# Fixing the order of all five queues in branch B of the long sequence

## The chip, the cores and the metric

The kernel runs on one core of one Trainium2 chip. The metric is the device time of one launch in microseconds (us), from runs on the chip. Engines are named as the profile names them: PE is TensorE (PEld its weight loads), DVE VectorE, ACT ScalarE, POOL GpSimd, SP SyncE, which here only issues DMAs. A name with a q (SPq, ACTq) is the queue that issues a DMA.

## What is computed

One layer of an encoder with two token mixers, for two sequences, a short one of 512 tokens and a long one of 1024, each of width 1024:

```python
xn = _rmsnorm(x, norm_mix_g)
z  = xn @ w_in                      # -> q_A k_A v_A q_B k_B v_B gate_A gate_B
o_a = gqa_attention(...)            # branch A: all keys, rotary, 8 heads
o_b = neighbourhood_attention(...)  # branch B: tokens on a 64-wide grid, 8 rows x 16 columns
                                    # of keys around a query, a learned bias per head and offset
mix = (sigmoid(ga) * (o_a @ w_proj_a) + sigmoid(gb) * (o_b @ w_proj_b)) @ w_out
x = x + mix
x = x + relu(_rmsnorm(x) @ w_mlp_up)**2 @ w_mlp_down
```

and a last RMSNorm. All products are made in split form: each operand is a high part and a low part (the remainder), and a product is three matmuls (`mm3`). The high part is an ACT copy, the low part a DVE subtraction (`split`, here called a cut).

## The kernel before

`run` handles the short sequence (NB = 1), then the long one (NB = 2): phase R (projections of branch A), phase A (its attention), phase B (branch B's attention), phase G (gated merge and `w_out`). `mlp` follows for both. The change is in phase B of the long sequence.

Phase B goes in steps `i` of one unit each; a unit `u = (h, j)` is head `h` and strip `j` of 16 grid columns. There are `n = 32` units; the first 24 are `moved`: their probabilities are transposed by a detour through DRAM instead of on PE. What happens to a moved unit `u = units[i]`:

- step i: `s_unit` adds bias and mask (POOL, `bm`), computes the scores on PE into one of two big PSUM tiles, adds the bias and takes the minimum on DVE (L1049, below called the sums), then exp on ACT (L1075) into `pb`, of which there are two, and scales by 1/sum on POOL (L1078);
- step i+1: `turn`, a DVE transpose of 32x32 blocks (L1087), and `dump`, a DMA from ACT's queue to DRAM (`tbs<-pbs`, L1094);
- step i+2: `fetch_t`, four DMAs from SP's queue that bring the blocks back in turned order (`bhs<-tbs`, L1104);
- step i+3: `t_unit`, a high copy on ACT (L1115) and a low subtraction on DVE (L1116);
- step i+4: `v_unit`, six matmuls with the values into a PSUM tile (`obs`), then `finish_o`, which adds the two halves of that tile (ACT L470, DVE L471 and L483) and writes them to DRAM through `put`.

Between those, every step issues fill work on PE: pulls from the generator `gate` (three matmuls a pull, 16 pulls a chunk of 128 gate columns, tanh at the end of each half chunk), and in steps 5, 6 and 7 of every eight the projection `qkproj` of the next two heads. `prep_v` loads the value strips (SP, `vss<-vds`, L942). From step 25 on the fill is `proj_a`, the product with `w_proj_a` (`ppas`). Its first weights and its operands `oX` are loaded at step 21 and cut one after the other from the list `oa_held`, whose first entry (the cut of the first weight chunk, `w_pa`) is taken at the end of step 22.

PSUM has four tiles for everything but scores (`mm`): gate sums, projections, transposes and `obs` share them. Weight tiles of `proj_a` come from the left pool `s8l`, which has six slots; until branch B's gate is done, the six hold parts of the split input `xhl`, the first of them the first half of the first 512 tokens (`xs_0`, k = 0 to 3). Raw weights pass through three buffers (`rawp`).

The scheduler of the tile framework puts each engine's instructions in a queue order at compile time. Before the change PE's order was pinned to the source (`keep_in_program_order` while `held_pe` is set); on ACT, DVE and SP `note` and `behind` made a few instructions (exp, sums, fetches and strip loads) stay behind every cut or load traced since the last such point, and the rest was free. POOL was free.

Of the kernel before, what the change touches and what calls it, by code (L numbers as in the profile page):

```python
# [18 lines left out]
P = 128  # L19
D = 1024  # L20
NC8 = D // P
# [40 lines left out]
def encoder(ctx: ExitStack, tc: tile.TileContext, xs, outs, w):  # L62
# [120 lines left out]
    held_pe = []  # L183
    firm = {"ACT": [], "DVE": [], "SP": []}

    def note(engine, op):
        if held_pe:
            firm[engine].append(op.ins)

    @contextmanager  # L190
    def behind(engine):
        with ExitStack() as st:
            for ins in firm[engine]:
                st.enter_context(tc.issue_after(ins))
            yield
        firm[engine].clear()

    def split(hi, lo, src, pin=False):
        op = nc.scalar.activation(hi, src, AF.Copy)  # L199
        note("ACT", op)  # L200
# [4 lines left out]
        for a, b in zip(cut, cut[1:]):  # L205
            op = nc.vector.tensor_tensor(lo[:, a:b], src[:, a:b], hi[:, a:b].bitcast(F32), op=ALU.subtract)
            if pin:
                tc.keep_in_program_order(op)
            note("DVE", op)

    def mul(out, a, b, **kw):
        op = nc.tensor.matmul(out, a, b, **kw)  # L212
        if held_pe:
            tc.keep_in_program_order(op)
# [16 lines left out]
    def load_cols(src, off, ncol, name, alloc=None, pin=False, hold=None, raw_of=None):  # L231
# [9 lines left out]
        for k0 in range(0, nk, kp):  # L241
# [4 lines left out]
            note("SP", op)  # L246
# [172 lines left out]
    def run(tr, nxt, first):  # L419
# [19 lines left out]
        def gate(goff, dst, c0=0, c1=NC8):  # L439
# [3 lines left out]
            for c in range(c0, c1):  # L443
                wg = nxt_w
                held = []
                if c + 1 < c1:
                    nxt_w = load_cols(win, goff + (c + 1) * P, P, f"g{N}_{goff}_{c + 1}", hold=held)
# [393 lines left out]
        def load_o(br, hold=None, raw_of=raw_tile):  # L841
            parts = []
            for k in range(4 - br):
                raw = None

                def ask(k=k):
                    r = raw_of(f"rawo{N}_{br}_{k}")
                    note("SP", nc.sync.dma_start(r[:, :T], (oad, obd)[br][k * P : (k + 1) * P, :]))
                    return r
# [24 lines left out]
        def proj_a(pool, raw_of):  # L874
            nxt_w = load_cols(
                w["w_proj_a"][0], 0, P, f"pa{N}_0", slot_left, NB == 2, oa_held if NB == 2 else None, raw_of
            )
            oA = load_o(0, oa_held, raw_of)
            if NB == 1:
                oa_held.pop(0)()  # L880
            yield
            for c in range(NC8):
                wp = nxt_w
                if c + 1 < NC8:
                    nxt_w = load_cols(
                        w["w_proj_a"][0], (c + 1) * P, P, f"pa{N}_{c + 1}", slot_left, raw_of=raw_of
                    )
                else:
                    wp_b.append(load_cols(w["w_proj_b"][0], 0, P, f"pb{N}_0"))
                for tb in range(NB):  # L890
# [4 lines left out]
                    za = pool.tile([P, 512], F32, tag="za", name=f"za{N}_{c}_{tb}", bufs=2)  # L895
                    nc.sync.dma_start(za, zg[0][c * P : (c + 1) * P, cs])
                    for k in range(4):
                        while len(oa_held) > max(0, 2 - k):
                            oa_held.pop(0)()
                        mm3(p_, wp[k][0], wp[k][1], oA[k][:, 0, cs], oA[k][:, 1, cs], k == 0, k == 3)  # L900
# [3 lines left out]
                        mA[tb, c // 4][:, c % 4, :], za, 1.0, p_, op0=ALU.add, op1=ALU.mult  # L904
# [8 lines left out]
        with phase(f"phB{N}") as ph:  # L913
            msk = ph.tile([P, halves * 3, nkey], BF16, tag="msk", name=f"msk{N}", bufs=1)
            nc.gpsimd.dma_start(msk, w["mask2"] if halves == 2 else w["mask1"])
            rects, strips, bms, PT = {}, {}, {}, {}
# [38 lines left out]
            def qkproj(pr, wqk, dest):  # L955
# [4 lines left out]
                def queries(tb):  # L960
# [5 lines left out]
                    for e in range(2):  # L966
# [11 lines left out]
                        note("ACT", nc.scalar.activation(dst_h, src, AF.Copy, scale=0.125))  # L978
                        for jj in range(4):
                            op = nc.vector.scalar_tensor_tensor(  # L980
# [7 lines left out]
                            note("DVE", op)  # L988
# [29 lines left out]
            def s_unit(u, before=None):  # L1018
                h, j = u
                ct = (0, 1, 1, 2)[j]  # L1020
                c0 = (0, 8, 24, 32)[j]
                jr = (16, 8, 8, 0)[j]
                s = big(f"sb{N}_{h}_{j}")
                for hf in range(halves):
                    r0 = 0 if hf == 0 else 4
                    ir = 4 if hf == 0 else 0
                    if j != 2:
# [7 lines left out]
                        bms[hf] = bm  # L1035
                    q0 = j * (T // 4) + hf * P
                    so = s[:, hf * 512 : hf * 512 + nkey]
                    for i in range(2):
# [3 lines left out]
                        mul(so, qk[h // 2][0][:, h % 2, q0 : q0 + P], kv, start=(i == 0), stop=(i == 1))  # L1042
                sums = []
                for hf in range(halves):
# [3 lines left out]
                    with behind("DVE"):  # L1048
                        nc.vector.tensor_tensor_reduce(  # L1049
                            out=sb,  # L1050
                            in0=s[:, hf * 512 : hf * 512 + nkey],
                            in1=bms[hf],
                            op0=ALU.add,
                            op1=ALU.min,
                            scale=-1.0,
                            scalar=3e38,
                            accum_out=nm_,
                        )
                    sums.append((sb, nm_))
                if before is not None:  # L1060
                    before()
                ps = []
# [3 lines left out]
                for hf, (sb, nm_) in enumerate(sums):  # L1066
                    nm = f"{N}_{h}_{j}_{hf}"
                    l = sml.tile([P, 1], F32, tag="l", name=f"lb{nm}")
# [5 lines left out]
                    with behind("ACT"):  # L1074
                        nc.scalar.activation(to, of, AF.Exp, bias=nm_, scale=-1.0, accum_out=l)  # L1075
                    rl = sml.tile([P, 1], F32, tag="rl", name=f"rlb{nm}")
                    nc.vector.reciprocal(rl, l)
                    nc.gpsimd.tensor_scalar(p, p, rl, 1.0, op0=ALU.mult, op1=ALU.mult)  # L1078
                    ps.append(p)
                PT[u] = pm if u in moved else ps  # L1080

            def turn(u):
# [4 lines left out]
                tc.keep_in_program_order(nc.vector.transpose(blocks, blocks))  # L1087
# [891 lines left out]
```

## Time and profile before

| what | value |
|---|---|
| median of three runs | 2148.83 us (2147.6 to 2149.58) |
| profiled execution, its own time | 2150.11 us |
| its span, first to last instruction | 2148.2 us |
| mean granted PE clock | 0.995 |
| PE, DVE, ACT, POOL busy | 98%, 69%, 53%, 17% of the span |
| phase B of the long sequence, steps 0 to 33 | 798.6 to 1072.3 us |

Times in the trace count from the start of the span. An engine's idle time stands in brackets in a row of the timeline, with what ended it. The order of the steps on PE can be read from the scores (`sbs`), four matmuls at the head of each step: step 8 starts at 855.06, step 16 at 915.42, step 24 at 989.74, step 27 at 1026.11.

### The profile page before, as it was taken

The page shows a single profiled execution, that of the slowest core. Times are in us where ns is not written, and L with a number is a line of the kernel's source. Part 1 is how long each engine was busy: PE and PEld are TensorE (multiplying, and loading weights), DVE is VectorE, ACT ScalarE, POOL GpSimd, SP SyncE. Part 2 cuts the span into 40 slices and gives each one's busy share as a digit, 9 for nine tenths or more (in the row PEclk, how much of TensorE's full clock was granted, in tenths as well). Part 3 has the DMA queues.
Part 4 walks back from the last instruction along what each step waited for, and adds up shares of the span by engine and source line. Part 5 has one row for each costly group of instructions (what it writes and reads, how often), then busy time and mean ns, then how long its engine had stood idle before and what let it go on. Part 6 is the DMA issues. An engine that isn't in the chain of part 4 may idle for free.

```text
span 2148.2 us, 32018 instructions
## 1 busy us (share of the span) xinstructions
PE 2105.0 (98%) x10871; PEld 1842.7 (86%) x10871; DVE 1483.7 (69%) x2793; ACT 1143.3 (53%) x2487; POOL 359.8 (17%) x446
## 2 busy tenths in 40 slices
PE   9999999999999999997999999999999999999998
PEld 8888778988897888876888899999999988888886
DVE  6665786777657757666782877778777777759563
ACT  6664653767566645544540566566655643434352
POOL 2232310323233224423200200003000000000000
PEclk9999999999999999999999999999999999999999
DMA  6437557520222146576562665578444799788561
GB/s 190 133 98 206 159 162 248 187 69 26 62 75 66 42 108 191 180 211 180 178 225 111 213 196 179 181 236 218 152 154 153 252 355 336 219 276 282 169 201 63
DMA packets 338538, 372.94 MB, mean 174 GB/s; under 512 B 33472, under 2 KB 269640, under 8 KB 338376
## 3 DMA queue, kind: packets, MB, share of 16 engines
q1 hardware_dynamic: 296695, 296.17, 44.3%
q10 hardware_dynamic: 34528, 54.55, 7.1%
q0 software_dynamic: 7152, 20.19, 3.6%
q8 instruction: 86, 1.41, 0.3%
q14 instruction: 77, 0.62, 0.1%
HBM read 274.29 MB, written 97.32 MB: 173 GB/s over the span
## 4 chain that ended last, share of the span: by engine, by line
PE 64%; DMA 2%; DVE 2%; ACT 1%; issue 1%; SPq 1%; POOL 0%; ACTq 0%; POOLq 0%; DVEq 0%
PE dn L212 20%; PE ua L212 6%; PE ud L212 6%; PE uc L212 6%; PE gpss L212 4%; PE ops L212 4%; PE ub L212 3%; PE ppbs L212 2%; PE ppas L212 2%; PE dnf L212 2%; PE pqbs L212 2%; PE pTs L814 1%; PE pkbs L212 1%; DMA tbs<-pbs 1%; PE obs L212 1%
## 5 line engine op out<-in xcount | busy, mean ns | idle before, releaser
L212 PE MATMUL dn<-wd,ah 128*128 128x512 f32 x1248 | 384.4, 389 | 0.0
L212 PEld LDWEIGHTS dn<-wd,ah 128*128 128x128 f32 x1248 | 234.3, 188 | 48.6
L212 PE MATMUL dn<-wd,al 128*128 128x512 f32 x624 | 242.8, 389 | 0.0
L1453 ACT ACTIVATE ah<-ar 128x512 fp32r<-128x512 f32 x168 | 104.4, 628 | 200.9 <-PE dn L212 188.3
L212 PE MATMUL gpss<-xs_0h,w_gs 128*128 128x512 f32 x512 | 188.4, 403 | 5.0 <-ACT w_gs L199 4.2
L1454 DVE TENSOR_TENSOR al<-ar,ah 128x512 fp32r<-128x512 f32 x168 | 114.3, 688 | 76.4 <-ACT ah L1453 66.6
L212 PE MATMUL ud<-B,A 128*128 128x384 f32 x768 | 143.6, 334 | 0.8 <-DVE c L1571 0.8
L212 PE MATMUL uc<-B,A 128*128 128x384 f32 x768 | 143.7, 334 | 0.0
L212 PE MATMUL ua<-B,A 128*128 128x384 f32 x768 | 138.8, 334 | 0.0
L212 PEld LDWEIGHTS dn<-wd,al 128*128 128x128 f32 x624 | 117.2, 188 | 24.2
L780 POOL TENSOR_SCALAR ps<-ps,rls 128x1024 f32<-128x1024 f32 (+1 forms) x96 | 97.2, 1014 | 225.3 <-DVE rls L779 199.9
L212 PEld LDWEIGHTS ud<-B,A 128*128 128x128 f32 x768 | 133.9, 188 | 1.1 <-DVE c L1571 1.1
L212 PEld LDWEIGHTS uc<-B,A 128*128 128x128 f32 x768 | 134.1, 188 | 0.2 <-ACT A L1453 0.2
L212 PEld LDWEIGHTS ua<-B,A 128*128 128x128 f32 x768 | 133.7, 188 | 0.2
L820 DVE TENSOR_TENSOR ptls<-pTs,pths 128x512 fp32r<-128x512 f32 x160 | 107.6, 686 | 37.5 <-ACT pths L819 36.9
L819 ACT ACTIVATE pths<-pTs 128x512 fp32r<-128x512 f32 x160 | 94.2, 598 | 73.8 <-PE pTs L814 71.3
L212 PE MATMUL ops<-wh_os,mgs 128*128 128x512 f32 x384 | 119.4, 390 | 0.0
L774 DVE TENSOR_REDUCE nms<-ss 128x1 f32<-128x1024 f32 (+1 forms) x96 | 99.9, 1041 | 25.5 <-PE ss L772 25.0
L212 PEld LDWEIGHTS gpss<-xs_0h,w_gs 128*128 128x128 f32 x512 | 96.1, 189 | 24.4 <-ACT w_gs L199 5.1
L777 ACT ACTIVATE ps<-ss,nms 128x1024 f32<-128x1024 f32 (+1 forms) x96 | 93.3, 973 | 22.7 <-DVE nms L774 20.1
L180 POOL TENSOR_TENSOR rs_f<-ms_f,mhalf 128x1 f32<-128x1 f32 x6 | 4.0, 668 | 590.7 <-DVE ms_f L176 590.7
L814 PEld LDWEIGHTS pTs<-ident,ps 128*128 128x128 f32 x640 | 77.9, 140 | 28.6 <-POOL ps L780 4.5
(287 smaller groups left out, 5147.9 us busy)
## 6 DMA issues: line engine op xcount, KB each, us to landing
ar<-ud SPq DMA_DIRECT2D x120, 512.0 KB, 4.7
br<-in_w_mlp_down_dram SPq DMA_DIRECT2D x72, 512.0 KB, 5.1
rawu<-in_w_mlp_up_dram SPq DMA_DIRECT2D x64, 512.0 KB, 4.1
ud<-c ACTq DMA_DIRECT2D x128, 192.0 KB, 3.0
raw_gs<-in_w_in_dram SPq DMA_DIRECT2D x32, 512.0 KB, 4.0
ud<-cs SPq DMA_DIRECT2D x64, 192.0 KB
tbs<-pbs ACTq DMA_DIRECT2D x24, 384.0 KB, 3.8
bhs<-tbs SPq DMA_DIRECT2D x96, 96.0 KB, 2.9
```

Of the source, the lines that this page charges most:

```text
L180: nc.gpsimd.tensor_tensor(r[:, :n], m[:, :n], mhalf[:, :n], op=ALU.pow)
L212: op = nc.tensor.matmul(out, a, b, **kw)
L774: nc.vector.tensor_reduce(nm_, s, axis=AX.X, op=ALU.max, negate=True)
L777: nc.scalar.activation(p, s, AF.Exp, bias=nm_, accum_out=l)
L780: nc.gpsimd.tensor_scalar(p, p, rl, 1.0, op0=ALU.mult, op1=ALU.mult)
L814: nc.tensor.transpose(pt[:, j * P : (j + 1) * P], PP[u, j][:, kc * P : (kc + 1) * P], ident)
L819: nc.scalar.activation(hi, pt, AF.Copy)
L820: nc.vector.tensor_tensor(lo, pt, hi.bitcast(F32), op=ALU.subtract)
L1453: nc.scalar.activation(hi, src, AF.Copy)
L1454: nc.vector.tensor_tensor(lo, src, hi.bitcast(F32), op=ALU.subtract)
```

## The change

The notes and the pins of phase B go. A new function, `in_order`, is called at the end of every step and once after the loop; it adds to each instruction traced since its last call an order edge (no semaphore) behind the one traced before it on the same engine. So from the first step on PE, ACT, DVE, POOL and SP each issue in the order in which the source names them, DMA issues included. The source is rearranged with that:

- `s_unit` is split in `bias_sums`, `scores`, `sums`, `exps` and `scale`; in the long sequence the biases of unit i+1 are added in step i, and the dump stands directly behind the exp.
- `finish_o` of a `v_unit` is kept in a list `ends` and traced in the next step, behind that step's exp and scale.
- On SP a step now holds, in this order: fetches, puts of the step before, rectangles, value strips, weights.
- The cut of the next gate chunk moves from the third k of the chunk's first half to the second k of its second half.
- `proj_a` asks for weights up to three chunks ahead and cuts them one chunk ahead; `za` is asked for one half chunk ahead.
- In the steps from 22 on, the entry of `oa_held` at the end of a step comes before the `v_unit`s, not behind.
- The short sequence keeps its loop, written apart, with the same order in it.

The core of the diff:

```diff
+    def in_order(start=False):
+        traced = nc.cur_bb.bb.instructions
+        if start:
+            firm.append(traced[-1])
+            return
+        k = next(k for k in reversed(range(len(traced))) if traced[k] is firm[0])
+        for ins in traced[k + 1 :]:
+            if ins.engine in chained:
+                tc.add_manual_dep(ins, chained[ins.engine].name, ... NoSync ...)
+            chained[ins.engine] = ins
+        firm[0] = traced[-1]
...
-                        if k == 2:
-                            while held:
-                                held.pop(0)()
+                        if k == (1 if firm else 2) and tb == (NB - 1 if firm else 0):
+                            while cuts:
+                                cuts.pop(0)()
...
         def proj_a(pool, raw_of):
+            ask_w(0)
+            if NB == 1:
+                cut_w(0)
+            else:
+                oa_held.append(partial(cut_w, 0))
             oA = load_o(0, oa_held, raw_of)
+            if NB == 2: (entries 2 and 3 of oa_held also call ask_w(1), ask_w(2))
...
                     for k in range(4):
                         while len(oa_held) > max(0, 2 - k):
                             oa_held.pop(0)()
+                        if NB == 2 and k == 1:
+                            if (c, tb) != (NC8 - 1, 1):
+                                ask_z(c + tb, 1 - tb)
+                            if tb == 0:
+                                cut_w(c + 1)
+                                if c + 3 <= NC8:
+                                    ask_w(c + 3)
                         mm3(p_, wp[k][0], wp[k][1], oA[k][:, 0, cs], oA[k][:, 1, cs], k == 0, k == 3)
...
+            for i in range(n + 2 if NB == 2 else 0):
+                slot_no[0] = i
+                f = (8, 7, 7, 6, 6, 0, 0, 4)[i % 8] if i < n - 8 else 8
+                if i == n - 11:
+                    pa = proj_a(ph, raw_here)
+                    next(pa)
+                late = 0 < i <= n and units[i - 1] in moved
+                if i < n:
+                    parts = sums(u, scores(u))
+                    if late:
+                        turn(units[i - 1])
+                    parts = exps(u, parts)
+                    if late:
+                        dump(units[i - 1])
+                    if i + 1 < n:
+                        bias_sums(units[i + 1])
+                    scale(u, parts)
+                while ends:
+                    ends.pop(0)()
+                if i > 1 and i < n + 2 and units[i - 2] in moved:
+                    fetch_t(units[i - 2])
+                while later_put and later_put[0][0] < i:
+                    nc.sync.dma_start(*later_put.pop(0)[1:])
+                if i < n:
+                    (prep_bias, prep_v, qkproj, load_qk: as before)
                 if i == n - 7:
                     for u in due_v.pop(i):
                         v_unit(u)
                     fill.drain()
                     fill.add(pa)
                 fill.pull(f // 2)
                 for u in due_t.get(i, ()):
                     t_unit(u)
+                (held cuts of qkproj's weights, oa_held from step 23, rest of qkproj)
                 fill.pull(f - f // 2)
+                if oa_held and i >= n - 10:
+                    oa_held.pop(0)()
                 for u in due_v.get(i, ()):
                     v_unit(u)
+                in_order()
```

More of the change, by code (lines that the diff above doesn't have):

```diff
@@ L1034, in s_unit, with scores @@
                         )
-                        bms[hf] = bm
+                        last_bm[hf] = bm
+                    bms[u, hf] = last_bm[hf]
+            def scores(u):
+                h, j = u
+                c0 = (0, 8, 24, 32)[j]
+                s = big(f"sb{N}_{h}_{j}")
+                for hf in range(halves):
+                    r0 = 0 if hf == 0 else 4
                     q0 = j * (T // 4) + hf * P
@@ L1047, in s_unit, with exps @@
                     nm_ = sml.tile([P, 1], F32, tag="nm", name=f"nmb{nm}")
[L1048 to L1062, printed above, removed]
+                    nc.vector.tensor_tensor_reduce(
+                        out=sb,
+                        in0=s[:, hf * 512 : hf * 512 + nkey],
+                        in1=bms.pop((u, hf)),
+                        op0=ALU.add,
+                        op1=ALU.min,
+                        scale=-1.0,
+                        scalar=3e38,
+                        accum_out=nm_,
+                    )
+                    res.append((sb, nm_))
+                return res
+            def exps(u, parts):
+                h, j = u
                 pm = ph.tile([P, halves * nkey], F32, tag="pb", name=f"pb{N}_{h}_{j}", bufs=4 // halves)
@@ L1180, in run @@
             held = []
-            if moved:
-                slot_no[0] = 0
-                held_pe.append(1)
-                fill.pull(3)
             due_t, due_v = {}, {}
```

247 lines of the change are left out of this document (137 added, 110 removed).

## The prediction

> **What bounds the kernel now.** I read the page's busy shares first, then the table of busy time by stretch, cut at the scores of steps 0, 8, 16, 24 and 27 of the loop.
>
> ```profile
> PE 2105.0 (98%) x10871; PEld 1842.7 (86%) x10871; DVE 1483.7 (69%) x2793; ACT 1143.3 (53%) x2487; POOL 359.8 (17%) x446
> ...
> core 0: us, PE busy (x) PEld busy (x) DVE busy (x) ACT busy (x) POOL busy (x), PEclk, DMA share, GB/s
> 798.61:855.06 56.45, 56.45 (x268) 48.03 (x267) 37.62 (x96) 28.94 (x60) 25.07 (x30) 1.00 0.67 191
> 855.06:915.42 60.36, 59.61 (x291) 50.89 (x291) 43.40 (x111) 32.10 (x64) 25.37 (x30) 1.00 0.60 180
> 915.42:989.74 74.32, 65.20 (x290) 53.89 (x290) 45.92 (x108) 35.42 (x66) 20.14 (x26) 0.93 0.69 205
> 989.74:1026.11 36.37, 28.70 (x130) 22.80 (x129) 23.34 (x54) 15.55 (x34) 11.96 (x14) 0.91 0.56 169
> 1026.11:1072.32 46.21, 46.21 (x235) 39.28 (x235) 39.27 (x97) 25.61 (x56) 10.96 (x14) 1.00 0.60 180
> ```
>
> PE is the bound and is kept supplied, except in two stretches. Steps 8 to 15 and 16 to 23 issue the same matmuls (x291, x290), but take 60.36 and 74.32 us. With the 0.75 that PE idles in the first (60.36 - 59.61), steps 16 to 23 lose 74.32 - 59.61 = 14.7 us. For steps 24 to 26 I count the work from these pieces of the chain:
>
> ```profile
> 911.97 2.72 PE gpss L212 x12
> 914.69 0.73 PE obs L212 x6
> 915.42 0.72 PE sbs L212 x4
> ...
> 1020.95 0.66 PE ptbs L1125 x6
> 1021.60 2.77 PE ppas L212 x12
> ```
>
> Twelve wide matmuls are four pulls. The steps hold 27 pulls (18.5), three scores (2.2), four value products (2.9) and two units of transposes (1.3): 24.9 of the 36.37, so 11.4 lost. In all 0.75 + 14.7 + 11.4 = 26.9 us, which is what the change can win here. The Trainium skill (Perfetto Trace Analysis, Identifying the Most-Contended Engine) says that matmul busy time is a bad measure of the room left. The trace agrees: by PE's idle time alone the two stretches would lose 9.1 + 7.7 = 16.8.
>
> The timeline of PE shows where, with the idle time in brackets:
>
> ```profile
> 931.49 0.50 PE L212 MATMUL gpss<-xs_0h,w_gs 128*128 128x512 f32 x1 [0.84 <-ACT w_gs L199]
> 949.28 0.80 PE L212 MATMUL gpss<-xs_0h,w_gs 128*128 128x512 f32 x1 [3.36 <-ACT w_gs L199]
> 962.26 0.50 PE L212 MATMUL pkbs<-xs_0h,w_bks 128*128 128x512 f32 x1 [0.92 <-ACT w_bks L199]
> 975.02 0.97 PE L212 MATMUL obs<-bhs,vss 128*128 128x256 f32 x6 [4.01 <-issue]
> 999.24 0.99 PE L212 MATMUL obs<-bhs,vss 128*128 128x256 f32 x6 [1.70 <-DVE bhs L1116]
> 1015.92 5.03 PE L212 MATMUL ppas<-oXs,w_pas 128*128 128x512 f32 x12 [5.18 <-ACT w_pas L199]
> ```
>
> The rest of the 26.9 is clock: after the 3.36 of idle time the granted clock is half,
>
> ```profile
> 949.30:953.50 4.20, 4.20 (x14) 3.87 (x15) 4.20 (x11) 1.99 (x6) 2.32 (x3) 0.50 0.58 177
> ```
>
> and the twelve matmuls behind the 5.18 took 5.03 instead of 2.77, 2.3 more. Three of these waits are cuts of weights. Their loads stand in the chain:
>
> ```profile
> 925.81 4.55 DMA raw_gs<-in_w_in_dram
> 930.38 1.07 ACT w_gs L199
> 931.48 1.29 DVE w_gs L206 x2
> ...
> 943.90 4.25 DMA raw_gs<-in_w_in_dram
> ...
> 965.41 6.43 DMA tbs<-pbs
> ...
> 1010.13 5.08 DMA raw_pas<-in_w_proj_a_dram
> ```
>
> The three weight loads were issued 5.4 to 5.8 us ahead of the matmul that wants them and take 4.3 to 5.1 to land, and the cut comes on top. They left late because SP stood before fetches that waited for their dumps (13 waits):
>
> ```profile
> SPq L1104 <- DMA tbs<-pbs: 50.0, 13, 6.5
> ```
>
> **The change part by part.** It adds no instruction and no semaphore; each edit moves something.
>
> 1. *Gate loads and cuts.* The load stays at the head of a chunk on PE, but on SP it now stands behind that step's fetches, puts and strips alone. The cut comes seven pulls later, 7 x 0.68 = 4.8 us, so SP may be that much later before ACT waits, and six pulls (4.1) remain for the cut's 1.07 + 1.29. This takes the waits at 931.49 and 949.28 with their clock. If SP fell behind by more than that, both would be back.
>
> 2. *Cuts of `qkproj`'s weights and the evacuations.* The 0.92 is a cut that the source has in step 20 and PE wants in step 22; it now runs where it stands. The 4.01 at 975.02 has no releaser ("issue"); PE wanted a PSUM tile there, and ACT, which empties them, had stood before an exp that waited for the dump of 965.41. With the steps before it no longer late and bunched, two dumps no longer follow each other closely, so I let this wait go.
>
> For 1 and 2 the bounds are 0 (nothing of the 0.75 + 14.7 is won) and 15.5. I take 14.0: the loads have their lead, and 1.5 stay for waits in the short steps (3 and 4 of each eight), as the 0.75 of steps 8 to 15 shows that one can occur.
>
> 3. *The first cut of `w_pa`, in step 22.* This speaks against the change. The left pool is full of `xhl` until the gate's last read of `xs_0`, which comes in the third of the four pulls of step 23. The trace shows it:
>
> ```profile
> 975.83 1.41 PE L212 MATMUL sbs<-kBs,qBs 128*128 128x384 f32 x4
> 985.75 0.42 DVE L483 TENSOR_TENSOR os_Bs<-ot_Bs 64x256 f32<-64x256 f32 x1
> 987.12 0.88 DVE L980 SCALAR_TENSOR_TENSOR qBs<-pqbs,qBs 64x128 fp32r<-64x128 f32 x4 [0.95 <-ACT qBs L978]
> 988.11 0.61 PE L212 MATMUL gpss<-xs_0h,w_gs 128*128 128x512 f32 x2
> 988.65 0.63 ACT L199 ACTIVATE w_pas<-raw_pas 128x512 fp32r<-128x512 f32 x1
> 989.38 0.76 DVE L206 TENSOR_TENSOR w_pas<-raw_pas,w_pas 128x256 fp32r<-128x256 f32 x2
> 990.16 0.56 DVE L1049 CUSTOM_DVE_ANT_0 sbss<-sbs,bms 128x384 f32<-128x384 f32 x1
> ```
>
> The last read starts at 988.11, the cut at 988.65, and the sums of step 23, whose scores were done at 977.24 (first row), ran at 990.16, held behind it. Before, only the sums were held; ACT emptied PSUM meanwhile. In source order everything of step 23 on ACT and DVE is queued behind this cut, and on SP the load that reuses its raw buffer with step 23's fetches behind that. On PE, gate, `pkb`, `obs` of unit 18 and `pqb` hold the four PSUM tiles, and the `v_unit` at the end of step 23 needs one. It gets it from `finish_o` of unit 18, which stands behind exp and dump. By these durations and those above
>
> ```profile
> L1049 DVE CUSTOM_DVE_ANT_0 sbss<-sbs,bms 128x384 f32<-128x384 f32 x64 | 33.7, 547 | 6.2 <-PE sbs L212 6.0
> L1075 ACT ACTIVATE pbs<-sbss,nmbs 128x384 f32<-128x384 f32 x64 | 39.0, 610 | 31.8 <-DVE nmbs L1049 19.4 <-DMA tbs<-pbs 11.7
> L470 ACT ACTIVATE ot_Bs<-obs 64x512 f32<-64x512 f32 x32 | 19.0, 595 | 43.1 <-PE obs L212 36.7 <-DVE os_Bs L483 6.0
> L471 DVE TENSOR_TENSOR ot_Bs<-obs,ot_Bs 64x512 f32<-64x512 f32 x32 | 21.8, 680 | 31.6 <-ACT ot_Bs L470 31.5
> L1004 DVE TENSOR_TENSOR kBs<-pkbs,kBs 64x512 fp32r<-64x512 f32 x36 | 24.7, 687 | 22.4 <-ACT kBs L1002 21.8
> ```
>
> the chain is cut 0.63, low part 0.76, sums 0.55, two exps with their accumulator reads 1.6, the dump's issue 0.3, L470 0.60, L471 0.68: 5.1 us after the last read. PE has one pull (0.7) left, so it waits 4.4. Then the scores of step 24 need the new heads' `qB` and `kB`, cut behind that on DVE: L483 (0.4), three of L1004 (2.1), half of `qB` (0.9): 8.5 after the read, PE being there at 5.8, so 2.7 more. DVE then has the other half of `qB`, a `t_unit`, two `oX` cuts (2.6) and step 24's own work before the `t_unit` of unit 21, near 18; PE wants that at the head of step 25, 8.5 + 8 pulls (5.5) + scores and values (2.2) and the slow clock = 18: 0.5 at most. Half a clock behind the 4.4 costs the 2.3 seen at 1015.92. And PSUM tiles of `obs` are freed later (next part): 1.8 over steps 25 and 26, an estimate of 0.9 a step: L471 and a short wait before it. Sum 4.4 + 2.7 + 0.5 + 2.3 + 1.8 = 11.7. Bounds: 0 if a slot is free in time, 17.5 if the 4.4 and 2.7 are half as long again and the clock is lost twice.
>
> By the Trainium skill (TensorE: Matmul & The Clock Gate, What's actually happening) the clock halves after about 3.4 us idle and needs as long busy to return. By it the half clock would cost 1.7 here, and a wait of under 3.4 none; the row's 0.50 behind 3.36 us agrees, and I keep the 2.3 measured.
>
> 4. *`finish_o` a step later.* It takes ACT 0.60 and DVE 0.68 + 0.41 from the end of a step and puts them behind the next exp, some 4 us later. The tile of `obs` is held that long. In steps with one `obs` and `qkproj` four tiles do, as counted above. From step 25 on two projections, two transposes and one or two `obs` share the four: bounds 0 and 4.0 (the one wait for a tile shown, 4.01), I take 1.0 for steps 27 to 33, which have no idle time now.
>
> 5. *`proj_a`'s loads ahead.* They take the 5.18 with its 2.3, the waits behind `oX` (0.7) and the 1.70 of steps 24 to 26, all of the 11.4; the new losses there are part 3. The raw buffers go round three at a time as before.
>
> 6. *Biases a unit ahead, puts earlier, dump ahead of the reciprocals, `za` ahead*: POOL is busy 20.14 of 74.32 us and SP's strips are needed four steps later, so 0; if POOL's order failed, the sums would wait 1 us a step for L1029.
>
> Sum, against the profiled execution's 2150.11: -14.0 (parts 1 and 2), -11.4 + 11.7 = +0.3 (3 and 5), +1.0 (4): -12.7. That execution is 1.3 above the median of the three runs; from the median, 2148.83 - 12.7 = 2136.1, or 2136.
>
> **The rivals.** *No block at step 22*: the pool gives a slot in time, or ACT gets through step 23 without PE noticing. For it: ACT had other work until just before 988.65, so that row alone does not prove what the cut waited for. Against it: the sums behind it, 13 us late, and that it starts within 0.2 us of the read's end (988.11 and one pitch of 0.23, the duration of 0.39 behind it). The 11.7 of part 3 falls away: 2124.
>
> *Slower: the ring of dump and exp.* There are two `pb`, so the exp of unit i waits for the dump of unit i-2 to land, and ACT, now in strict order, issues the dump of i-1 behind that exp:
>
> ```profile
> tbs<-pbs ACTq DMA_DIRECT2D x24, 384.0 KB, 3.8
> ```
>
> One unit takes at least landing + 0.3 + 1.6. With the median of 3.8 that is 5.7, just under the mean of 8.0 of steps 0 to 23 (191.1 / 24). It decides from a landing of 6.0 on: as slow as before. With the 6.43 of the chain's worst, 8.4 x 24 = 201, so 10 slower there, with parts 3 to 5 +11: 2160. Against it: it must hold for all dumps, and 3.8 is the median.
>
> *Little changes: the waits move.* SP's 50 us before fetches remain in the source's order, each now with everything behind it, so gate weights come late again, and a stop of ACT at a cut holds exp and evacuation. Then of the 14.0 some 0 to 5 are won: 2145 to 2150. Against it: the cut's seven pulls.
>
> **How the numbers follow.** Chances: forecast 0.52, no block 0.23, little changes 0.15, slower ring 0.10. A change of 0.2% (4.3 us) is about what a measurement of this kernel can tell. The first two are faster; of the third 0.05 faster, 0.07 the same and 0.03 slower; the fourth is slower. So 0.80 faster, 0.07 the same, 0.13 slower. The forecast's own range is 2130 to 2143 (parts 1, 2 and 4 at their bounds within reason, part 3 by 4 either way). The range to 2122 takes in the second case, up to 2148 most of the third, and leaves out the ring.
>
> **What would show it.** Right: no idle time of PE before `gpss` or `pkbs` behind `w_gs`, `w_bks`; steps 16 to 23 in 65 us or less; `ppas` never waits for `w_pas`; at the end of step 23 a wait of 4 to 5 before `obs` and of 2 to 3 before `sbs`, with the `w_pas` cut on ACT just behind the last read of `xs_0`, and ACT idle for 8 us or more ahead of it. Wrong: that cut earlier, or exps far behind their sums throughout with "DMA tbs" as what ended the wait, or gate weights that still land behind their need.

## The result, and the profile after

The changed kernel takes 2169.4 us (median of 4 runs, 2167.35 to 2172.07) beside 2149.2 for the kernel before on the same chip (4 runs, 2147.6 to 2149.61): ratio 1.0096, 95% interval 1.0079 to 1.0114. That is 20 us slower, where 13 us faster was forecast. The profiled execution took 2170.12 us, its span is 2168.3.

The page's busy times and the table by stretch, cut as in the prediction at the scores of steps 0, 8, 16, 24 and 27, and now on into the next phase, whose first product (`ppbs`) starts at 1091.05:

```profile
PE 2113.9 (97%) x10871; PEld 1846.2 (85%) x10871; DVE 1490.3 (69%) x2793; ACT 1142.6 (53%) x2487; POOL 363.4 (17%) x446
```

```profile
core 0: us, PE busy (x) PEld busy (x) DVE busy (x) ACT busy (x) POOL busy (x), PEclk, DMA share, GB/s
798.44:856.24 57.80, 56.78 (x268) 47.97 (x267) 38.21 (x100) 28.58 (x60) 22.84 (x30) 1.00 0.63 190
856.24:924.44 68.20, 63.03 (x291) 52.80 (x291) 48.74 (x112) 34.86 (x68) 29.08 (x30) 0.95 0.73 206
924.44:996.36 71.92, 62.61 (x292) 52.45 (x290) 46.41 (x105) 32.38 (x65) 25.89 (x29) 0.95 0.66 195
996.36:1037.33 40.97, 31.85 (x129) 25.23 (x128) 27.37 (x59) 18.20 (x34) 11.45 (x13) 0.83 0.59 170
1037.33:1092.00 54.67, 50.90 (x240) 40.82 (x239) 38.79 (x94) 25.77 (x56) 9.62 (x14) 0.97 0.44 129
```

Every stretch but one is longer: 57.80, 68.20, 71.92 and 40.97 stand against 56.45, 60.36, 74.32 and 36.37 before. Nearly all of the loss lies in this loop: from the scores of step 0 to the first `ppbs` it took 273.7 us before and takes 292.7 now, which is 19.0 of the 20.1 by which the span grew. PE does the same matmuls. Its timeline shows the new idle times in brackets:

```profile
898.40 0.79 PE L214 MATMUL pkbs<-xs_0h,w_bks 128*128 128x512 f32 x1 [3.65 <-DVE ot_Bs L470]
958.12 0.49 PE L214 MATMUL pqbs<-xs_0h,w_bqs 128*128 128x512 f32 x1 [2.23 <-DVE ot_Bs L470]
994.77 1.62 PE L214 MATMUL obs<-bhs,vss 128*128 128x256 f32 x6 [4.34 <-issue]
998.60 0.98 PE L1074 MATMUL sbs<-kBs,qBs 128*128 128x384 f32 x2 [1.27 <-DVE qBs L1008]
1021.52 5.49 PE L214 MATMUL ppas<-oXs,w_pas 128*128 128x512 f32 x12 [5.13 <-DVE mAs L931]
1043.35 4.61 PE L214 MATMUL ppas<-oXs,w_pas 128*128 128x512 f32 x12 [1.25 <-DVE ot_Bs L470]
```

No matmul waits for `w_gs`, `w_bks` or `w_pas` any more; in that the change does what it was made for. But other waits took their place, above all of three kinds: for PSUM tiles that `finish_o` empties (L470), for the new heads at step 24, and for the product that empties a projection (L931). On ACT, the waits of exps for their sums grew from the first row (before) to the second (after):

```profile
ACT pbs L1075 <- DVE nmbs L1049: 19.4, 17, 2.8
```

```profile
ACT pbs L1110 <- DVE nmbs L1084: 65.4, 25, 11.2
ACT w_pas L203 <- PE gpss L214: 8.6, 1, 8.6
```

**How the 3.65 comes about.** The timelines of SP, ACT and DVE around step 13 of the changed kernel, whose scores ended at 887.9:

```profile
883.52 0.45 SPq L1299 DMA_DIRECT2D obds<-os_Bs  x1
884.01 3.60 SPq L970 DMA_DIRECT2D vss<-vds  x4
887.72 0.40 SPq L245 DMA_DIRECT2D raw_gs<-in_w_in_dram  x1
...
892.40 1.06 ACT L203 ACTIVATE w_gs<-raw_gs 128x1024 fp32r<-128x1024 f32 x1 [3.66 <-DMA raw_gs<-in_w_in_dram]
895.30 0.62 ACT L1110 ACTIVATE pbs<-sbss,nmbs 128x384 f32<-128x384 f32 x1 [1.84 <-DVE nmbs L1084]
...
893.49 1.29 DVE L209 TENSOR_TENSOR w_gs<-raw_gs,w_gs 128x512 fp32r<-128x512 f32 x2 [2.73 <-ACT w_gs L203]
894.71 0.55 DVE L1084 CUSTOM_DVE_ANT_0 sbss<-sbs,bms 128x384 f32<-128x384 f32 x1
897.66 0.68 DVE L470 TENSOR_TENSOR ot_Bs<-obs,ot_Bs 64x512 f32<-64x512 f32 x1 [0.86 <-ACT ot_Bs L469]
```

SP issues the load at 887.72, behind a put and four strips. ACT reaches the cut in its held order and stands 3.66 us; DVE stands before the low part; the sums of step 13 run 7 us after their scores (2.7 of it is idle time of DVE, the rest other work that stands ahead of them), then the exp, then `finish_o`, and only then is the tile free that `pkb` wants at 894.75. Behind this wait the granted clock is 0.50 from 898.40 to 903.00, and half of these 4.6 us, an estimate, is lost on top of it. In the kernel before, the same load left at 878.62 and ACT cut it at 886.10 without a wait:

```profile
878.62 0.45 SPq L245 DMA_DIRECT2D raw_gs<-in_w_in_dram  x1
...
886.10 1.05 ACT L199 ACTIVATE w_gs<-raw_gs 128x1024 fp32r<-128x1024 f32 x1
```

### The profile page after: what moved, and what is told of

It reads as the page before. It is cut to its first block, busy times and chain, and to the rows that moved or that the text cites. A ratio compares the mean times of both kernels' runs of the same rounds, so it can differ in the third digit from the quotient of the medians.

```text
span 2168.3 us, 32021 instructions
## 1 busy us (share of the span) xinstructions
PE 2113.9 (97%) x10871; PEld 1846.2 (85%) x10871; DVE 1490.3 (69%) x2793; ACT 1142.6 (53%) x2487; POOL 363.4 (17%) x446
## 4 chain that ended last, share of the span: by engine, by line
PE 60%; DVE 4%; DMA 3%; ACT 2%; issue 1%; SPq 0%; POOL 0%; ACTq 0%; DVEq 0%; POOLq 0%
PE dn L214 19%; PE ua L214 6%; PE ud L214 6%; PE uc L214 6%; PE ops L214 4%; PE gpss L214 3%; PE ub L214 3%; PE ppbs L214 2%; PE dnf L214 2%; PE pTs L813 1%; PE ppas L214 1%; PE pkbs L214 1%; PE pqbs L214 1%; PE os L790 1%; PE os L789 1%
## 5 line engine op out<-in xcount | busy, mean ns | idle before, releaser
L819 DVE TENSOR_TENSOR ptls<-pTs,pths 128x512 fp32r<-128x512 f32 x160 | 107.7, 687 | 37.3 <-ACT pths L818 36.4
L776 ACT ACTIVATE ps<-ss,nms 128x1024 f32<-128x1024 f32 (+1 forms) x96 | 93.2, 972 | 22.8 <-DVE nms L773 20.1
```

The source lines that it names most:

```text
L776: nc.scalar.activation(p, s, AF.Exp, bias=nm_, accum_out=l)
L819: nc.vector.tensor_tensor(lo, pt, hi.bitcast(F32), op=ALU.subtract)
```

## The experiments

All runs in one table. Stretches are read from the starts of the scores and of the first `ppbs` in one profiled execution each; among the three kernels with the same code up to step 24 (e8, e15, e16) they differ by up to 2.2 us. The kernel before measured 2148.1 to 2148.9 beside the experiments, and each ratio is to its runs on the same chip. The intervals are 4 to 8 us wide, so a difference of 2 or 3 us between two experiments is not shown by their medians alone.

| kernel | median us | ratio to before, 95% | 0-7 | 8-15 | 16-23 | 24-26 | 27 to ppb |
|---|---|---|---|---|---|---|---|
| before | 2149.2 | | 56.4 | 60.4 | 74.5 | 36.2 | 46.2 |
| after | 2169.4 | 1.0079-1.0114 | 57.7 | 68.2 | 71.9 | 41.0 | 53.9 |
| e1 finish_o at once | 2169.3 | 1.0082-1.0112 | 60.6 | 69.4 | 75.0 | 37.3 | 50.5 |
| e2 w_pa cut later | 2157.3 | 1.0028-1.0053 | 57.7 | 66.2 | 68.0 | 35.1 | 52.3 |
| e3 only PE held | 2159.0 | 1.0036-1.0070 | 56.5 | 64.8 | 79.0 | 34.9 | 46.6 |
| e4 SP free | 2160.9 | 1.0042-1.0072 | 57.2 | 66.5 | 71.5 | 34.7 | 52.3 |
| e5 gate loads on POOL | 2164.7 | 1.0059-1.0089 | 58.9 | 63.0 | 73.5 | 40.2 | 52.3 |
| e6 dumps on POOL | 2166.9 | 1.0070-1.0100 | 59.8 | 64.9 | 67.5 | 42.4 | 53.9 |
| e7 za on POOL | 2168.6 | 1.0075-1.0109 | 57.9 | 68.2 | 73.4 | 40.5 | 51.8 |
| e8 = e2+e5+e7 | 2151.7 | 1.0003-1.0022 | 58.6 | 63.0 | 65.8 | 32.6 | 52.1 |
| e9 = e8, finish_o mid-step | 2156.8 | 1.0028-1.0055 | 58.6 | 63.2 | 65.8 | 33.9 | 58.4 |
| e11 gate cut early | 2188.7 | 1.0178-1.0206 | 68.1 | 74.2 | 77.3 | 40.0 | 52.3 |
| e12 = e2+e3 | 2160.6 | 1.0046-1.0074 | 56.4 | 64.4 | 80.9 | 36.8 | 46.4 |
| e14 DVE free | 2162.2 | 1.0050-1.0081 | 58.6 | 66.9 | 69.1 | 36.5 | 51.1 |
| e15 = e8, DVE free in the tail | 2151.9 | 1.0005-1.0023 | 60.5 | 63.0 | 67.7 | 33.8 | 51.7 |
| e16 = e15, ACT free there too | 2148.2 | 0.9990-1.0008 | 60.3 | 63.1 | 68.0 | 34.6 | 47.2 |
| e10 before + new proj_a | 2145.9 | 0.9979-0.9997 | 56.4 | 60.4 | 73.6 | 32.9 | 46.1 |
| e13 = e10, gate loads on POOL | 2142.9 | 0.9964-0.9986 | 56.4 | 59.4 | 72.1 | 32.6 | 46.1 |

Two theories stood at the start. BANK: `finish_o` a step later holds PSUM tiles. QUEUE: in a held order one late load stops ACT, then DVE, then the emptying of PSUM.

**e1, e2: part 4 undone; the `w_pa` cut later.**

```diff
-                if NB == 2:
-                    ends.append(partial(v_end, u, o))
-                else:
-                    v_end(u, o)
+                v_end(u, o)
```
```diff
-                if oa_held and i >= n - 9:
+                if oa_held and i >= n - 8:
...
-                if oa_held and i >= n - 10:
+                if oa_held and i >= n - 9:
```

> The changed kernel with finish_o traced right behind its v_unit again, at the end of the step; all five queues stay in source order. Theory BANK (finish_o behind the next step's exp keeps the obs tile in PSUM, so PE waits for one of four tiles): the waits of PE that end with L470 go (1.02, 3.65, 2.23, 1.25, 1.52 and smaller ones, about 11 us, with clock 14), so about 2155 against 2169; pkb at step 14 does not wait. Theory QUEUE (a late load on SP stops ACT at a cut, and behind it DVE and all evacuation, wherever finish_o stands): within 4 us of the changed kernel, 2165 to 2171, with the same places waiting for another releaser.

> The changed kernel with the entries of oa_held taken half a step later, so that the first cut of w_pa stands behind the gate's last read of xs_0 (end of step 23 instead of 22). By the step of the prediction on this cut, the 8.6 us that ACT waits for gpss goes, with PE's 4.3 before obs and 1.3 before sbs and their clock: 6 to 9 us faster than the changed kernel, 2160 to 2163. If it is worth nothing because the oX cuts and raw buffers then come too late for ppas, within 2 us, 2167 to 2171, with a longer wait before the first ppas.

e1 gained nothing in the whole, as QUEUE said: the waits behind L470 shrank to 2.0 us, others (for `bhs`, `mAs`, `kBs`) grew by as much. BANK as the one cause falls.

e2 won 12.1 us, more than the 6 to 9 expected (its eight runs spread from 2150.59 to 2162.68). The 4.34 and the 1.27 are gone, and so is a wait that the expectation left out, the 5.13 before `ppas`. In the changed kernel SP stands before a load until the low part of `w_pa` frees a raw buffer (first row, 10.8 us in one wait), so the first loads of `za`, which the product `mAs` needs, leave only 20.9 us after the scores of step 24 (1017.04). In e2, where the longest of these waits is 6.1, the first leaves 17.4 after them (1007.21), and the wait for `mAs` is 0.40 (second row). Part of this is paid back: `ppas` waits 4.5 for `oX` in e2.

```profile
SPq L847 <- DVE w_pas L209: 19.8, 3, 10.8
```

```profile
1011.12 3.94 PE L214 MATMUL ppas<-oXs,w_pas 128*128 128x512 f32 x12 [0.40 <-DVE mAs L931]
```

**e3, e4: which queues are held.** `in_order` chains only the engines named.

```diff
         for ins in traced[k + 1 :]:
+            if ins.engine not in (PE,):        # e3; in e4 (PE, Activation, DVE, Pool)
+                continue
```

> The changed kernel's source, but in_order holds PE's queue alone; ACT, DVE, POOL and SP are laid by the scheduler. QUEUE: the coupling goes, and the rearranged source (later cuts, loads ahead) is worth what was forecast: 2135 to 2148. BANK: the tiles are held as long as the scheduler puts finish_o late, so 2155 to 2169.

> The changed kernel with SP's queue alone left to the scheduler, the four others in source order. If the loads that come late are SP's strict order (QUEUE, SP's part): raw_gs lands before its cut at step 13, ACT does not stop there, 8 us or more faster, 2150 to 2161. If SP is late for its own load (some ten issues of 0.45 us a step and the waits for dumps), which no order mends: within 4 us, 2165 to 2173. BANK: the same as the changed kernel.

Either won some half of the loss, but neither as expected. e3's 2159.0 lies in the range given for BANK, not in QUEUE's 2135 to 2148, though no matmul waits for `finish_o` in it. With PE alone held the last steps are as short as before (46.6), while weights come late (6.13 and 2.93 for `w_gs`, 8.4 in all for `w_bks`). So the rearranged source, with PE alone held as it was before the change, is 11 us slower than the kernel before (interval 8 to 15); these are other waits than those of the changed kernel, where no matmul waits for these weights.

e4 is at the edge of QUEUE's range, but by another way: the gate load of step 13 leaves at 886.55, only 1.2 earlier than in the changed kernel, ACT still stands 3.26 at the cut and `pkb` waits 3.21. In e3 the load leaves at 885.49. So the held order of SP is not what makes this load late. What e4 won lies mostly in steps 24 to 26, where the wait for `mAs` fell to 1.14.

**e5, e6, e7, e8: single transfers taken off SP or ACT, and three edits together.** In e5 the gate's load in the loop, in e6 the dump, in e7 the load of `za` is issued by `nc.gpsimd`; e8 has e2, e5 and e7.

```diff
-            op = nc.sync.dma_start(rv, v[...])              # e5: q = nc.gpsimd for the gate
+            op = (q or nc.sync).dma_start(rv, v[...])
-                nc.scalar.dma_start(PT[u], pm...)           # e6
+                nc.gpsimd.dma_start(PT[u], pm...)
-                nc.sync.dma_start(zas[c, tb], zg[0][...])   # e7
+                nc.gpsimd.dma_start(zas[c, tb], zg[0][...])
```

> The changed kernel with the gate's weight loads issued by POOL instead of SP, at the same place of the source. QUEUE (SP, held in source order, comes to the load a step late: it issued the one for step 13 at 887.72, so ACT stood idle 3.66 us at the cut and everything of step 13 on ACT and DVE behind it): the load goes out by 883, ACT does not wait at the cut, the 3.65 us wait of pkbs at 898.40 is under 1, steps 8 to 15 take 62 to 63 us instead of 68.20, the whole 2162 to 2164. BANK (the wait comes from finish_o holding PSUM and from the place of the cut, whenever the data lands): pkbs still waits 2 us or more there, steps 8 to 15 stay at 66 or more, the whole 2167 to 2170.

> The changed kernel with the dumps issued by POOL instead of ACT. In the changed kernel puts and strips on SP wait for dumps that they have nothing to do with (prep_v for tbs<-pbs 15.7 us in 7 waits, a put 2.8). QUEUE: these waits on SP go, the gate load of step 13 goes out 3 us or more earlier, steps 8 to 15 take 62 to 65 us, the whole 2160 to 2166. Rival: POOL comes to the dump behind its multiplication, 1 to 2 us later, the fetch lands later and the values wait for bhs: 2170 to 2180, with obs behind bhs as the wait that grows.

> The changed kernel with the loads of za issued by POOL instead of SP. QUEUE (za was issued at 1017.04 only, because SP stood 10.8 us before a load into a raw buffer that DVE had not yet cut; ppas waited 5.13 for mAs behind it and ran 5.49 at half clock): the 5.13 and the slow twelve go, 6 to 7.5 us less, the whole 2162 to 2164. BANK (the last steps lose by PSUM tiles that finish_o frees late, 0.4 to 1.5 each, whose clock is half): the wait moves to the next tile, 0 to 2 us less, the whole 2167 to 2170.

> The cut of w_pa half a step later (as measured, 12 us less), the gate loads on POOL and the loads of za on POOL, all in the changed kernel. QUEUE: the losses are separate, 12 + 6 + 6: 2145 to 2149, no slower than the kernel before. If they are the same microseconds met in another place: 2153 or more.

e5: steps 8 to 15 fell from 68.2 to 63.0, as QUEUE said; ACT cut `w_gs` at 888.72 without a wait, and the 3.65 became 1.40, not under 1. The whole fell by 4.7, a little less than QUEUE gave. So it is the late load that stops ACT there. e6: the waits of strips and puts for dumps went entirely, the gate load of step 13 left at 882.33, and steps 8 to 15 fell to 64.9; but exps and values waited for dumps and fetches instead, and 2.5 us remained of it, just above what QUEUE gave. e7 was a miss: 0.8, as BANK's range had it, but the wait did not move to another tile. POOL, held too, came to `za` behind its multiplication at 1016.29 instead of SP's 1017.04, and PE waited 5.68. With the early cut of `w_pa` in place `za` is late in either held queue; with the later cut PE waits 0.40 for `mAs` at that place in e2 (SP) and not at all in e8 (POOL). e8 won 17.7 of the 20. That lies between the two ranges given, which took 6 each for the gate loads and `za`, but it is the sum of what e2, e5 and e7 measured (17.6), as separate losses would give.

**e11, e12: is it the held order?** In e11 the gate's cut stands seven pulls earlier, where it was; e12 is e3 with e2's edit.

```diff
-                        if k == (1 if firm else 2) and tb == (NB - 1 if firm else 0):
+                        if k == 2 and tb == 0:
```

> The changed kernel with the gate's cuts back where they were in the source (third pull of the first half of the chunk, seven pulls earlier), everything else held in source order. QUEUE (in a held order a cut that stands ahead of its data stops ACT and with it DVE): ACT now waits at several cuts, 2 to 5 us each, 2172 to 2185; the late place of the cuts was right and the load was wrong. Rival CUT (the late cuts meet those of w_bq and w_bk and the sums of steps 12 to 15 on DVE, and this is the loss): steps 8 to 15 go under 65 us, 2160 to 2165.

> The changed kernel with the order held on PE only, and the cut of w_pa half a step later. PE alone held gave 2159.0, the later cut with all five held 2157.3. QUEUE (the early cut costs because everything on ACT and DVE is queued behind it): with ACT and DVE free to go round it there is little left to win, 2155 to 2160. If the cut costs by itself, whatever the queues: the two add, 2146 to 2150.

Both went the way QUEUE said, e11 further than its range and e12 to just above it. Moving the gate's cuts ahead cost 19 us more, and steps 8 to 15 grew to 74.2, so the rival CUT falls: by the waits of e11, ACT now stands at five of them, 29.6 us in all, 9.7 the longest. The rows below are that stop on ACT and PE's wait behind it:

```profile
ACT w_gs L203 <- DMA raw_gs<-in_w_in_dram: 29.6, 5, 9.7
```

```profile
901.23 1.06 ACT L203 ACTIVATE w_gs<-raw_gs 128x1024 fp32r<-128x1024 f32 x1 [9.69 <-DMA raw_gs<-in_w_in_dram]
...
907.12 0.79 PE L214 MATMUL pqbs<-xs_0h,w_bqs 128*128 128x512 f32 x1 [9.94 <-ACT sgs L459]
```

And the edit that won 12.1 with five queues held won nothing (2160.6 against 2159.0) with PE alone held, where ACT, left free, stands only 0.48 at that cut (e3). The early place costs by what is queued behind it.

**e9, e14, e15, e16: the last steps.** In e9 `finish_o` stands behind the first half of the pulls from step 25 on; in e14 DVE is not chained at all; in e15 and e16 DVE, or DVE and ACT, are not chained from step 25 on. e9, e15 and e16 stand on top of e8.

```diff
-                while ends:                                  # e9
+                while ends and i < n - 7:
...
                 fill.pull(f // 2)
+                while ends and i >= n - 7:
+                    ends.pop(0)()
```
```diff
         for ins in traced[k + 1 :]:
+            if ins.engine in free:       # e15: (DVE,), e16: (DVE, Activation), if i >= n - 7
+                continue
```

> The kernel of the late cut with gate loads and za on POOL (2151.7), and from step 25 on finish_o stands behind the first half of the step's pulls instead of ahead of them. ORDER (on DVE the product that empties the first projection's PSUM tile, ready near 1020.8, ran at 1025.53, because two finish_o with their round trips to ACT stand ahead of it; the next projection waits for that tile, 1.2 to 1.3 a step, and twelve matmuls take 3.0): steps 27 to 29 go from 10.1, 10.5 and 9.8 to 8.5 or less, 4 to 6 us less, the whole 2146 to 2148. TILES (four PSUM tiles are too few from step 25 on, whoever empties first): obs is held longer, ptbs waits for it instead, the whole 2151 to 2155.

> The changed kernel with the order held on PE, ACT, POOL and SP, and DVE free. DVE ORDER (the evacuation of a PSUM tile whose work is done stands behind other work in DVE's held order): steps 27 to 33 take 7.6 to 8.3 us each instead of 8.4 to 12, the waits of pkbs, pqbs, ptbs and ppas behind L470 go to under 2 us in all from 10.6, the whole 2158 to 2162. If ACT's held order costs as much by itself, since every finish_o and every cut goes through ACT first: 2165 to 2170.

> The kernel with the late cut and gate loads and za on POOL (2151.7), and DVE free from step 25 on only. DVE ORDER: steps 27 to 29, 10.1, 10.5 and 9.8 us there, take 8.3 or less, 5 to 7 us less, the whole 2145 to 2147. If the last steps lose by ACT's order or by the number of PSUM tiles: 2150 to 2153.

> As the run with DVE free from step 25 on (2151.9, steps 28 to 33 at 9.0, 9.5, 8.5, 9.2 and 9.0), with ACT free there too; PE, SP and POOL stay held. If the two held orders together make the last steps slow (finish_o is a chain that goes ACT, DVE, ACT, DVE, and in a held order nothing passes it on either): steps 27 to 31 take 7.6 to 8.3, as where PE alone is held, 6 to 8 us less, the whole 2144 to 2147. If it is SP's order or the place of finish_o a step later: 9 us a step as before, 2150 to 2153.

ORDER fell in e9: the tail grew to 58.4, PE now waiting for L931 in nearly every step, and the whole was slower than TILES had it too. The number of tiles alone is not the cause either: the kernel before and e16 have the same four and take 46.2 and 47.2. e14 took 2162.2, at the edge of what DVE ORDER gave, but its tail stayed at 51.1 and the waits behind L470's line at 8.9 us in all, not under 2. Rows of e8 for step 27, PE and then DVE, show what every place of `finish_o` runs into:

```profile
1021.69 0.52 PE L1166 MATMUL ptbs<-ident,pbs 128*128 128x128 f32 x3 [0.44 <-DVE ot_Bs L470]
1023.45 3.06 PE L214 MATMUL ppas<-oXs,w_pas 128*128 128x512 f32 x12 [1.25 <-DVE ot_Bs L470]
...
1022.71 0.68 DVE L470 TENSOR_TENSOR ot_Bs<-obs,ot_Bs 64x512 f32<-64x512 f32 x1 [0.72 <-ACT ot_Bs L469]
1024.33 0.42 DVE L479 TENSOR_TENSOR oXs<-os_Bs,oXs 64x256 fp32r<-64x256 f32 x1 [0.48 <-ACT oXs L478]
1025.53 0.68 DVE L931 SCALAR_TENSOR_TENSOR mAs<-zas,ppas 128x512 f32<-128x512 f32 x1
```

`finish_o` goes ACT, DVE, ACT, DVE. In a held order nothing passes it while it waits for the other engine, so the product of a projection whose matmuls ended near 1020.8 runs at 1025.53. DVE free alone (e15) changed nothing; DVE and ACT free (e16) brought the tail to 47.2, about as with PE alone held (46.6) and as before (46.2), and the whole to 2148.2, a little above the range given. So with ACT held the tail stays long. Whether ACT free alone would do was not run, and e16 frees all work of the two engines, not `finish_o` alone.

**e10, e13: the part that helps, without the held order.** e10 is the kernel before with the new `proj_a`; e13 also has e5's edit.

> The kernel before with the new proj_a alone: weights three chunks ahead with their cuts placed, za a half chunk ahead; all queues ordered as before. If the loads ahead are worth what the prediction gave them, the 5.18 before ppas, its half clock and the small waits of steps 24 to 26 go: 11.4 us less, the whole 2136 to 2139. Rival: the loads start no earlier, since the raw buffers and SP come free when they did, or the waits turn into waits for oX: 0 to 3 us less, 2145 to 2149.

> The kernel before with the new proj_a (2145.9) and its gate loads issued by POOL instead of SP; no queue held beyond what was held before. SP (the late gate weights of steps 18 and 20 come from SP standing before fetches, not from the place of the cuts): the waits of gpss for w_gs, 3.2 us here, and the half clock behind them go, steps 16 to 23 take 66 to 69 us instead of 73.5, the whole 2138 to 2142, faster than both kernels. Rival: the wait of obs at the end of step 22 (5.19, no releaser) stays and takes the place of what is won: 2144 to 2147.

e10 won 2.6 us (interval 0.6 to 4.5), as its rival had it: the 5.18 before `ppas` is gone, but `ppas` waits 2.1 for `oX`, and the wait before `obs` at step 22 became 5.19. e13, the fastest of all, beats both kernels: 5.4 us under the kernel before (interval 3.0 to 7.7). No matmul waits for `w_gs` any more. Its steps 16 to 23 and 24 to 26, and the waits before `obs`:

```profile
core 0: us, PE busy (x) PEld busy (x) DVE busy (x) ACT busy (x) POOL busy (x), PEclk, DMA share, GB/s
...
913.25:985.32 72.07, 62.47 (x293) 51.81 (x292) 47.37 (x109) 35.10 (x66) 23.58 (x28) 0.98 0.70 211
985.32:1017.94 32.62, 27.44 (x129) 22.20 (x128) 23.96 (x57) 16.63 (x35) 12.72 (x14) 0.95 0.65 187
```

```profile
PE obs L212 <- issue: 8.7, 4, 3.9
```

But steps 16 to 23 keep 72.07 where 66 to 69 was expected: as the rival there said, waits before `obs` (four, without a releaser, 8.7 in all against one of 5.2 in e10) took the place of the gate's. What `obs` waits for was not settled.

## Why the prediction was wrong

**Parts 1 and 2 failed.** The step that failed is "the cut comes seven pulls later ... so SP may be that much later before ACT waits". SP was later than that. It issued the load at 887.72, 10.5 us after the chunk's first matmul (877.26); the kernel before had issued it 2.9 after that matmul (875.68 and 878.62). So SP was 7.5 later, against the 4.8 allowed. The waits at PE for `w_gs` did go; the stop went to ACT. Steps 8 to 15 lost 7.8 us (60.4 to 68.2), a loss that the bounds "0 (nothing ... is won) and 15.5" leave out, though part 3 had worked out what a stop of ACT in a held order does. Steps 16 to 23 won 2.6, although the 4.34 of part 3 lies in them. Together 134.9 became 140.1, and in e2, without the stop of part 3, 134.2. So parts 1 and 2 taken alone won about nothing instead of 14.0. The rival "little changes" named this mechanism, gate weights late again and a stop of ACT that holds exp and emptying, and its "0 to 5" of the 14.0 is what came out, but for the stop of part 3; it priced the mechanism as a gain not won, never as a loss.

The sign does not hang on these parts alone. Had they won 14.0, the 4.34 in step 23 and the 13.8 that the other stretches lost (1.3 in steps 0 to 7, 4.8 in 24 to 26, 7.7 from 27 on) would still have made the kernel slower.

**Part 3 was right in the mechanism.** Forecast were 4.4 before `obs`, 2.7 before `sbs`, the cut just behind the last read of `xs_0`, ACT idle for 8 or more, and 11.7 in all. Measured were 4.34, 1.27, 8.59 of idle time on ACT,

```profile
989.57 0.63 ACT L203 ACTIVATE w_pas<-raw_pas 128x512 fp32r<-128x512 f32 x1 [8.59 <-PE gpss L214]
991.62 0.62 ACT L1110 ACTIVATE pbs<-sbss,nmbs 128x384 f32<-128x384 f32 x1 [1.43 <-DVE nmbs L1084]
```

and 12.1 won back by moving that cut (e2). That the two sums agree is in part luck. The 12.1 holds the wait for `mAs`, which part 3 did not have: it said that SP's load of that raw buffer stands behind the cut, but put no price on what is late behind it.

**Part 4 was mis-sized.** The 1.0, with bounds 0 and 4.0, stands against 7.7 from step 27 on (46.2 to 53.9). The place of `finish_o` is not the main cause: with it undone (e1) the tail was still 50.5, and moving it (e9) made it longer. The held order is, that of ACT at least: the tail took 51.7 with DVE free there (e15) and 47.2 with both free (e16).

**Part 5 was mis-sized.** 11.4 was forecast, 2.6 measured by itself (e10). The sum took all of the loss in steps 24 to 26 as removable, down to 24.9 of counted work. No kernel came under 32.6 there, with PE busy 27.4.

**Part 6 put `za` at 0.** It was issued four pulls before its need and behind other work of its step; PE lost 5.13 there, and the twelve matmuls behind it took 5.49 instead of 2.77. Part of its lateness came from SP's stop of 10.8 behind the early cut of part 3, as e2 shows.

**The rival of the ring** had its condition met, a landing of dumps of 6.0 or more, but not its effect. The median landing rose from 3.8 to 6.1, yet exps waited for dumps 7.3 us in three waits, less than the 11.7 before:

```profile
tbs<-pbs ACTq DMA_DIRECT2D x24, 384.0 KB, 6.1
```

```profile
ACT pbs L1110 <- DMA tbs<-pbs: 7.3, 3, 2.6
```

Of the signs listed, right were: no matmul waits for `w_gs`, `w_bks` or `w_pas`, and step 23 as described, but for the wait before `sbs` (1.27, not 2 to 3). Wrong: steps 16 to 23 took 71.9, not 65 or less. Of the signs of failure, gate weights did land behind their need (ACT's 3.66), and exps did run far behind their scores, with late sums rather than the dump as the releaser.

## What to carry to other kernels

Here, with ACT and DVE held in source order, a late transfer became a stop of everything queued behind its cut on both engines, so the bound of a placed wait must reach below zero, and its price is that of the queue behind it. Before fixing an order, read for each cut when its load can leave its own queue: with the order left as it was, asking for `proj_a`'s loads earlier and taking the gate's loads off SP won 5 us (e13), where the change, which holds five queues, lost 20. Look hard at a chain that goes to and fro between two engines before holding its order: freeing both from step 25 on won back 4 to 5 us of the tail here, freeing DVE alone nothing.

## What was not expected of the hardware

**SP waits for transfers that it has nothing to do with.** The waits of SP's queue in the loop, changed kernel:

```profile
SPq L1299 <- DMA tbs<-pbs: 2.8, 1, 2.8
SPq L970 <- DMA tbs<-pbs: 15.7, 7, 3.7
```

Neither the put (L1299) nor the strips (L970) read or write `tbs`. With the dumps on POOL (e6) only the fetches that read `tbs` wait for it:

```profile
SPq L1146 <- DMA tbs<-pbs: 42.6, 12, 7.8
```

So here a transfer on SP waited for an unrelated dump when ACT had issued that dump, and not when POOL had. This is not the work of the change: in the kernel before strips wait for dumps nearly as long.

```profile
SPq L942 <- DMA tbs<-pbs: 13.5, 5, 8.7
```

Why is not shown.

**The clock can fall after a short wait.** Behind the 1.25 at 1043.35 (and 0.43 just before it) the granted clock fell in the changed kernel, to 0.63 over twelve matmuls (0.50 from 1044.50 to 1047.00):

```profile
1041.59:1043.35 1.76, 0.52 (x3) 0.28 (x4) 1.01 (x3) 0.59 (x1) 0.00 (x0) 1.00 0.00 0
1043.35:1047.96 4.61, 4.61 (x14) 3.67 (x15) 3.11 (x7) 1.81 (x4) 0.00 (x0) 0.63 0.16 43
```

The twelve matmuls took 4.61 instead of 2.77, and the same in e6 behind 0.44 and 1.25. In e8 the same waits, 0.44 and 1.25, left it at full speed:

```profile
1023.45:1026.51 3.06, 3.06 (x14) 2.42 (x15) 2.47 (x6) 1.81 (x4) 0.00 (x1) 1.00 0.37 107
```

The Trainium skill (TensorE: Matmul & The Clock Gate, What's actually happening) has the clock fall after about 3.4 us idle. The first two of these rows disagree: 1.7 us of idle time in 2.2 were followed by 0.63. What tells the two cases apart is not shown.
